# A softmax bound by its transfers: one late load issued 25 rows later, and a row over 126 and 2 partitions moved from the second load to the first store

## The chip, the cores and the metric

The kernel runs on one core of a Trainium2 chip. The metric is device time in microseconds (us); a profile shows the span of the core, about 1.3 us shorter. All runs quoted are of the state fast, and the granted clock of the profiled ones is 1.0. A few executions of the kernel before take 161.1 to 161.6 us instead of about 160.3 (6 of the 44 on record); they count as they are.

## The reference

```python
def reference(x):                       # x: 16 x 1024 x 512, float32
    x_scaled = x / 2.0
    x_max = np.max(x_scaled, axis=-1, keepdims=True)
    exp_x = np.exp(x_scaled - x_max)
    return (exp_x / np.sum(exp_x, axis=-1, keepdims=True)).astype(np.float32)
```

33.55 MB go in and 33.55 MB come out. Per partition there are 128 rows of 512 floats (2,048 B).

## The kernel before

The rows are cut into eight tiles of 3, 5, 15, 25, 25, 25, 20 and 10 rows per partition. The kernel's buffer in SBUF, the on-chip memory, holds 98 rows per partition, so tiles 6 and 7 take the places of tiles 0 to 3 once those are stored. ScalarE takes the exponential of a row and its sum, VectorE multiplies by the reciprocal, SyncE issues the stores. (The kernel's second path, with the maximum taken off, does not run on this data.)

```python
TILES = [(3, 0), (5, 3), (15, 8), (25, 23), (25, 48), (25, 73), (20, 0), (10, 20)]  # rows, place
LATE = {6: (0, 1, 2), 7: (3,)}      # late load: the stores that it waits for
SPREAD = 1
TURN = 73

def load(eng, t):
    r = tiles[t][1]
    parts = [(0, P, 0, r)]
    if t == SPREAD:
        parts = [(0, P, 0, r - 1), (0, 126, r - 1, r), (126, P, r - 1, r)]
    for p, q, lo, hi in parts:
        eng.dma_start(out=sb(t)[p:q, lo:hi], in_=dram(xf, t)[p:q, lo:hi]).then_inc(ld[t], 16)

def store(eng, t):
    eng.wait_ge(s_mul, upto[t])
    eng.dma_start(out=dram(of, t), in_=sb(t)).then_inc(sem_of.get(t, s_end), 16)
# ... ScalarE:
exponentials(straight, TURN)
for t, us in LATE.items():
    nc.scalar.wait_ge(s_home[t], landings(us))
    load(nc.scalar, t)
exponentials(TURN, n_rows)
```

## Time and profile before

| | before |
|---|---|
| time, median of 4 runs | 160.31 us (159.86 to 160.5) |
| span of the profile | 158.9 us |
| bytes moved, mean rate | 67.13 MB, 422 GB/s |
| late loads issued at | 72.9 and 101.0 us |
| last three stores issued at | 122.9, 134.8 and 140.7 us |

The prediction below shows the lines that carry this. Two things help in reading them. The row "DMA" has the busy tenths of the 16 DMA engines in 40 slices. And in the lists of DMA queues, q1 is the ring of SyncE (load 0 and all stores), q10 that of ScalarE (the other loads).

### The profile page before, as it was taken

The numbers are of one execution on the slowest core, as the hardware profiler recorded it, in microseconds if no ns is written. First come the engines' busy times: TensorE is split into PE (matmuls) and PEld (weight loads), VectorE is DVE, ScalarE is ACT, GpSimd is POOL, SyncE is SP. The second block draws the span as 40 slices with busy tenths as digits, with TensorE's granted clock in tenths as the row PEclk, the third lists the DMA queues.
The fourth block names the chain that finished last, engine by engine and source line by source line (L and its number), as shares of the span: only waits on it lengthen the run. The fifth ranks groups of instructions, "written<-read, shape, count | busy, mean of one in ns | idle before, by whom it ended". The sixth has DMA issues, their size and how long they took to land. (4 is left out here: it accounts for less than half of the span.)

```text
span 158.9 us, 665 instructions
## 1 busy us (share of the span) xinstructions
PE 0.2 (0%) x2; PEld 0.1 (0%) x2; DVE 75.1 (47%) x43; ACT 80.3 (51%) x257; POOL 0.2 (0%) x4
## 2 busy tenths in 40 slices
PE   0000000000000000000000000000000000000000
PEld 0000000000000000000000000000000000000000
DVE  0056008920499922989400000007899999960000
ACT  0870498009998089990000000399999999100000
POOL 0000000000000000000000000000000000000000
DMA  7999999799699998999999898997999999999996
GB/s 267 392 487 419 487 462 439 304 477 495 294 410 459 454 510 351 438 428 412 425 480 456 371 552 356 397 541 340 449 418 405 505 412 412 412 454 402 464 387 275
DMA packets 2450, 67.13 MB, mean 422 GB/s; under 512 B 272, under 2 KB 272, under 8 KB 656
## 3 DMA queue, kind: packets, MB, share of 16 engines
q1 hardware_dynamic: 1296, 34.34, 50.5%
q10 hardware_dynamic: 1152, 32.77, 48.4%
q14 instruction: 2, 0.02, 0.0%
HBM read 33.55 MB, written 33.55 MB: 422 GB/s over the span
## 5 line engine op out<-in xcount | busy, mean ns | idle before, releaser
L274 ACT ACTIVATE arena<-arena x125 | 76.6, 614 | 50.6 <-ACTq L135 50.6
L167 DVE TENSOR_TENSOR arena<-arena,recip 128x2560 f32<-128x2560 f32 (+2 forms) x19 | 71.3, 3752 | 0.7
L164 DVE RECIPROCAL recip<-stats 128x5 f32<-128x5 f32 (+2 forms) x19 | 3.7, 195 | 63.1 <-ACT arena L274 57.9
L274 ACT ACTIVATION_READ_ACCUMULATOR arena<-arena x125 | 23.3, 187 | 0.0
L195 ACT ACT_TABLE_LOAD x1 | 1.3, 1283 | 4.7 <-issue 4.7
L199 ACT ACTIVATE arena<-arena 128x512 f32<-128x512 f32 x3 | 1.9, 618 | 0.0
L160 DVE MEMSET ones<- 128x1 f32 x1 | 0.1, 59 | 2.7 <-PEq L35 2.7
L199 ACT ACTIVATION_READ_ACCUMULATOR arena<-arena 128x1 f32 x3 | 0.6, 186 | 0.0
L191 PE MATMUL total<-ones,count 128*1 128x1 f32 x2 | 0.2, 164 | 141.5 <-DVE count L179 141.5
L176 DVE TENSOR_TENSOR inside<-inside,stats 128x128 f32<-128x128 f32 x1 | 0.3, 291 | 0.0
L179 DVE TENSOR_REDUCE count<-inside 128x1 f32<-128x128 f32 x1 | 0.3, 285 | 0.0
L182 DVE TENSOR_SCALAR flag<-total 1x1 int32<-1x1 f32 x1 | 0.1, 147 | 0.3 <-PE total L191 0.3
L172 DVE TENSOR_SCALAR inside<-stats 128x128 f32<-128x128 f32 x1 | 0.2, 220 | 0.0
L191 PEld LDWEIGHTS total<-ones,count 128*1 128x1 f32 x2 | 0.1, 80 | 141.5 <-DVE count L179 141.5
L309 POOL MEMSET const-bfloat16-1.0<- 128x1 bf16 x1 | 0.1, 102 | 0.0
L309 POOL MEMSET const-uint8-127<- 128x1 uint8 x1 | 0.1, 102 | 0.0
L309 POOL MEMSET const-float32-1.0<- 128x1 f32 x1 | 0.1, 99 | 0.0
L309 POOL MEMSET const-float32-0.0<- 128x1 f32 x1 | 0.1, 98 | 0.2 <-issue 0.2
## 6 DMA issues: line engine op xcount, KB each, us to landing
arena<-in_x_dram ACTq DMA_DIRECT2D x3, 6400.0 KB, 52.3
out_dram<-arena SPq DMA_DIRECT2D x3, 6400.0 KB, 44.4
arena<-in_x_dram ACTq DMA_DIRECT2D x1, 5120.0 KB, 36.7
out_dram<-arena SPq DMA_DIRECT2D x1, 5120.0 KB, 18.1
arena<-in_x_dram ACTq DMA_DIRECT2D x1, 3840.0 KB, 15.0
out_dram<-arena SPq DMA_DIRECT2D x1, 3840.0 KB, 39.9
arena<-in_x_dram ACTq DMA_DIRECT2D x1, 2560.0 KB, 24.6
out_dram<-arena SPq DMA_DIRECT2D x1, 2560.0 KB, 18.2
```

Of the source, the lines that this page charges most:

```text
L160: nc.vector.memset(ones[:, :], 1.0).then_inc(s_ones, 1)
L164: nc.vector.reciprocal(out=recip[:, b : b + c], in_=stats[:, b : b + c])._wait_ge(s_exp, ks[-1] + 1).then_inc(s_rec, 1)
L167: nc.vector.tensor_mul(out=arena[:, a : a + c], in0=arena[:, a : a + c], in1=recip[:, b : b + c].unsqueeze(2).to_broadcast([P, c, D]),)._w ...
L172: nc.vector.tensor_scalar(out=inside[:, :], in0=stats[:, :], scalar1=LO, scalar2=HI, op0=Alu.max, op1=Alu.min,).then_inc(s_cnt, 1)
L176: nc.vector.tensor_tensor(out=inside[:, :], in0=inside[:, :], in1=stats[:, :], op=Alu.is_equal)._wait_ge(s_cnt, 1).then_inc(s_cnt, 1)
L179: nc.vector.reduce_sum(out=count[:, :], in_=inside[:, :], axis=mybir.AxisListType.X)._wait_ge(s_cnt, 2).then_inc(s_cnt, 1)
L182: nc.vector.tensor_scalar(out=flag[:, :], in0=total[:, :], scalar1=float(N), scalar2=float(n_rows // G), op0=Alu.is_ge, op1=Alu.mult,)._wa ...
L191: nc.tensor.matmul(total[:, :], lhsT=count[:, :], rhs=ones[:, :], start=True, stop=True)._wait_ge(s_cnt, 3).then_inc(s_tot, 1)
L195: nc.scalar.preload_act_table(Exp)
L199: ins = nc.scalar.activation(out=arena[:, b], in_=arena[:, b], func=Exp, scale=0.5, accum_out=stats[:, b : b + 1],)
L274: ins = nc.scalar.activation(out=data, in_=data, func=Exp, scale=0.5, accum_out=stats[:, r : n_rows - E + 1 + r][:, bass.ds(now, 1)],)
L309: nc = _bacc.Bacc("TRN2", target_bir_lowering=False, num_devices=1)
```

## The change

Load 7 used to be issued directly behind load 6, at row 73, and ScalarE stood still until store 3 had landed; now ScalarE first does tile 5 (rows 73 to 97). And the row that goes out in pieces of 126 and 2 partitions is one of store 0, no longer one of load 1.

```diff
-SPREAD = 1
-TURN = 73
+SPREAD = 0
+TURNS = {6: 73, 7: 98}
     def load(eng, t):
-        ... (three parts if t == SPREAD)
+        eng.dma_start(out=sb(t), in_=dram(xf, t)).then_inc(ld[t], 16)
     def landings(ts):
-        return 16 * len(list(ts))
+        return 16 * sum(3 if t == SPREAD else 1 for t in ts)
     def store(eng, t):
         eng.wait_ge(s_mul, upto[t])
-        eng.dma_start(out=dram(of, t), in_=sb(t)).then_inc(sem_of.get(t, s_end), 16)
+        parts = [(0, P, 0, r)]
+        if t == SPREAD:
+            parts = [(0, P, 0, r - 1), (0, 126, r - 1, r), (126, P, r - 1, r)]
+        for p, q, lo, hi in parts:
+            eng.dma_start(... [p:q, lo:hi] ...).then_inc(sem_of.get(t, s_end), 16)
-        exponentials(straight, TURN)
+        done = straight
         for t, us in LATE.items():
+            exponentials(done, TURNS[t])
             nc.scalar.wait_ge(s_home[t], landings(us))
             load(nc.scalar, t)
-        exponentials(TURN, n_rows)
+            done = TURNS[t]
+        exponentials(done, n_rows)
```

More of the change, by code (lines that the diff above doesn't have):

```diff
@@ L108, in load, with landings, store @@
     def load(eng, t):
+        eng.dma_start(out=sb(t), in_=dram(xf, t)).then_inc(ld[t], 16)
+    stored_by = {u: s_home[t] for t, us in LATE.items() for u in us}
+    for t, (_, r, at) in enumerate(tiles):
+        over = {u for u, (_, ru, au) in enumerate(tiles[:t]) if at < au + ru and au < at + r}
+        assert over <= {u for v, us in LATE.items() if v <= t for u in us}
+    def landings(ts):
+        return 16 * sum(3 if t == SPREAD else 1 for t in ts)
+    near = len(tiles) - 2
+    sem_of = {**stored_by, near: s_near}
+    at_end = landings(t for t in range(len(tiles)) if t not in sem_of)
+    def store(eng, t):
+        eng.wait_ge(s_mul, upto[t])
         r = tiles[t][1]
@@ L114, in load @@
             eng.dma_start(
-                out=sb(t)[p:q, lo:hi], in_=dram(xf, t)[p:q, lo:hi]
-            ).then_inc(ld[t], 16)
-    stored_by = {u: s_home[t] for t, us in LATE.items() for u in us}
-    for t, (_, r, at) in enumerate(tiles):
-        over = {u for u, (_, ru, au) in enumerate(tiles[:t]) if at < au + ru and au < at + r}
-        assert over <= {u for v, us in LATE.items() if v <= t for u in us}
-    def landings(ts):
-        return 16 * len(list(ts))
-    near = len(tiles) - 2
-    sem_of = {**stored_by, near: s_near}
-    at_end = landings(t for t in range(len(tiles)) if t not in sem_of)
-    def store(eng, t):
-        eng.wait_ge(s_mul, upto[t])
-        eng.dma_start(out=dram(of, t), in_=sb(t)).then_inc(sem_of.get(t, s_end), 16)
+                out=dram(of, t)[p:q, lo:hi], in_=sb(t)[p:q, lo:hi]
+            ).then_inc(sem_of.get(t, s_end), 16)
     def take(eng, sem, n):
@@ L188, in program @@
         for t in range(len(tiles)):
-            nc.tensor.wait_ge(ld[t], 48 if t == SPREAD else 16).then_inc(s_go, owner.count(t))
+            nc.tensor.wait_ge(ld[t], 16).then_inc(s_go, owner.count(t))
         nc.tensor.wait_ge(s_ones, 1)
```

## The prediction

> **What bounds the kernel now.** I read the page first, its list of engines and its row of DMA slices.
>
> ```profile
> PE 0.2 (0%) x2; PEld 0.1 (0%) x2; DVE 75.1 (47%) x43; ACT 80.3 (51%) x257; POOL 0.2 (0%) x4
> ...
> DMA  7999999799699998999999898997999999999996
> ...
> DMA packets 2450, 67.13 MB, mean 422 GB/s; under 512 B 272, under 2 KB 272, under 8 KB 656
> ...
> q1 hardware_dynamic: 1296, 34.34, 50.5%
> q10 hardware_dynamic: 1152, 32.77, 48.4%
> ```
>
> No compute engine is busy more than 51% of the 158.9 us span, and the two queues' packets together take 50.5 + 48.4 = 98.9% of the time of 16 DMA engines. q1 is SyncE's ring (first load and all stores), q10 ScalarE's (all other loads). The bound is the DMA engines. The packet records agree: laid over each other, they leave about 1.3 engine-averaged us without a packet in the first 4 us (1.02 of it before the first packet), about 0.1 us between 4 and 156 us, and 0.5 us of uneven finish at the end, with another 0.45 us from the last packet to the span's end. So all that any reordering could win back is about 2 us of 159, most of it at a start that the change hardly touches.
>
> Then the waits, because both halves of the change act on waits.
>
> ```profile
> DVE recip L164 <- ACT arena L274: 57.9, 8, 30.9
> ACT arena L274 <- ACTq L135: 50.6, 5, 30.3
> ```
>
> ScalarE idles once for 30.3 us. The timeline shows why:
>
> ```profile
> 72.92 28.37 ACTq L114 DMA_DIRECT2D arena<-in_x_dram  x2
> ...
> 101.81 0.63 ACT L274 ACTIVATE arena<-arena  x1 [30.26 <-ACTq L135]
> ```
>
> The two late loads, tiles 6 and 7, are issued one behind the other at row 73. ScalarE's order of instructions stands still between them, because tile 7 waits for the store of tile 3, which lands at about 101. Tile 5 (rows 73 to 97) had landed at 82.3 by the arrivals on its semaphore, so its exponentials are about 19 us late. But nothing runs dry for it: DMA stays at 9 or 8 tenths there. That long wait is not on the path that sets the end.
>
> Last, the packets by queue from 20 to 40 us:
>
> ```profile
> DMA packets 320, 8.65 MB, mean 432 GB/s; under 512 B 32, under 2 KB 32, under 8 KB 81
> ...
> q10 hardware_dynamic: 160, 7.37, 85.9%
> q1 hardware_dynamic: 160, 1.27, 15.1%
> ```
>
> Both queues served 160 packets, but q10 moved six times the bytes. A packet is one partition's run of one transfer (51,200 B for 25 rows, 6,144 for 3), and the queues alternate packet by packet. A store cut small therefore advances slowly beside a load of long runs.
>
> **What the Trainium skill says.** "DMA: Bandwidth & Descriptors", section "Queues, rings and completion order": each DMA engine round-robins between queue rows, at packet granularity. The equal 160 and 160 agree. Section "Why a DMA increments its semaphore by 16 and not by 1": the number of engines is the largest one up to 16 that divides the slowest dimension on both sides, and the lowest-numbered are taken; a DMA on fewer has the remainder added by the sequencer. So 126 partitions use 14 engines (9 packets each) and 2 partitions use 2. The trace agrees on the counts: load 1's semaphore has 34 arrivals, 16 + 14 + 2 from engines and two early ones from the sequencer; which engines they were it does not tell. Section "Where 436 GB/s comes from": 435.2 GB/s is the ceiling of the 16 ports. The trace fits: a 51,200 B packet takes about 1.89 to 1.93 us, 26.6 to 27.1 GB/s each, 425 to 434 for sixteen. At that ceiling 67.1 MB take 154.2 us, an estimate from the page, 4.7 under the span.
>
> **Part one: the spread row moves from load 1 to store 0.** Removed: two of ScalarE's first three DMA issues (0.66 and 0.24 us). Its table load, at 4.70, starts perhaps 1 us earlier, but the first exponential waits for load 0 (5.7), so at most 0.2 us is won there. Data costs per engine, with the mean time of a packet: load 1 now takes 8 x 315 + 8 x 88 ns = 3.22 us; in one piece, at the 385 ns that store 1's 10,240 B packets take, 3.08. Store 0 now takes 8 x 234 = 1.87 us; in pieces, 8 x 160 (estimate for 4,096 B at the same rate) + 8 x 88 = 1.98. Sum: -0.14 + 0.11 = -0.03 us. The packet totals even come out equal (q1 +144, q10 -144, 2,450 in all), and each engine's total bytes are the same before and after. Work of the bound: nothing.
>
> What moves is the order. Today store 0 has 8 packets per engine. After: 8 of two rows, plus 9 of one row on 14 engines (10 on two of them), 17 or 18, and still 8 on the two engines that the 126 rows leave out. Each takes a turn against a load packet. Its first turn comes at about 13.4; two rounds lie beside load 2's packets (1.13 + 0.16), the other 15 beside 51,200 B packets (1.9 + about 0.12 = 2.0):
>
> - Store 0 on 14 engines ends at 13.4 + 2.6 + 30 = 46, where it now ends at 27.4 (one engine at 29.7).
> - Store 1, 8 rounds of 1.89 + 0.385: 64, now 46 to 49.
> - By then 23 of the 24 packets of loads 3 to 5 are through on these engines, so store 2 runs alone: 8 x 1.14 = 9.1, plus the last load packet 1.9: 75 to 76, now 70.9 (one engine 72.9).
> - The two left-out engines keep today's schedule: there load 5 still ends at about 80, and a landing counts all 16. So loads 3, 4 and 5 land when they do now (35, 56, 82).
>
> Load 6, which waits for stores 0 to 2, is issued at about 76, not 72.9. SyncE's ring meanwhile holds store 3 (issued at 56.6) and, from 77.2, store 4, each 15.1 us of work for every engine, so none starves. Store 3, in rounds of 1.89 + 1.52 beside load 6, lands at about 101 as now.
>
> **Part two: load 7 at row 98.** ScalarE takes tile 5 as soon as it lands: 82.4 to 97.7 (25 x 0.612). Then store 3 is home at about 101, and load 7 is issued there, within 1 us of now: the row is no longer what holds it. Store 5 is issued at about 101.5, not 122.9. Load 6 lands at about 109.5: exponentials to 122, store 6 issued at 125 (now 134.8). Load 7 lands at about 125.5: its 10 rows take 6.1 us and VectorE 3 more, store 7 issued at about 134.8 (now 140.7). So VectorE's last work moves about 6 us ahead. But stores leave in ring order: store 6 now starts moving at 139.4 and store 7 at 151.5, 4.6 and 10.8 us after their issues. That slack is already there and now doubles. Gain at the end: 0. The one spot where the ring is now empty, 122.3 to 124.1 between stores 4 and 5, is covered by load 7's packets (idle 0.01 us). Gain there: 0.
>
> Sum: -0.03 us of packets, at most -0.2 at the start, up to +0.2 for more turns of tiny store packets: about -0.1. I take 160.3 us.
>
> **Rivals.** (1) A new wait: store 0's slow landing delays load 6 so much that the rings run dry. For it: store 0 gets over twice the turns and load 6 waits for it. Against: stores 3 and 4 stand in the ring from 56.6 and 77.2, so load 6 would have to come after 105 to leave a hole. It would cost the length of the hole; at a hole of 4 us, 164. (2) The opened chain pays: ScalarE's 30.3 us wait goes, VectorE's unbroken tail from 114 to 140.6 loosens, and the end comes earlier. For it: the chain that ended last goes through that tail. Against: the DMA slices stay full and stores 6 and 7 wait for the ring, not for VectorE. At best it gives the 0.5 us of uneven finish: 159.9. (3) The mix counts: 51,200 B loads took 1.91 to 1.93 us beside small stores and 1.89 beside large ones. Eight packets of load 5 moving from the second mix to the first on 14 engines cost 0.3 us: 160.7.
>
> **Range and chances.** A time outside 2% (under 157.3 or over 163.7) needs a hole of 3 us in a stream that has none, or more than all that idles today. 160.3, with 159.6 to 161.0 from the three runs' own spread (160.16 to 160.5), rivals 2 and 3 and some for another chip. Faster 0.01, same 0.97, slower 0.02.
>
> **What would show it.** q1 with 1,440 packets and q10 with 1,008, both shares still about 99% together; in the window 20 to 40 us q1's share down from 15% to about 7%. Store 0's last piece landing about 36 us after issue instead of 19.7, store 1 about 50 (34.2), load 6 issued at 75 to 77. ScalarE's longest wait down from 30.3 to 10 to 13 us, and store 7 issued at 133 to 137. If loads 3 to 5 land much earlier than 35, 56 and 82, the 126 rows were spread over all engines and my account of two unslowed ones is wrong. If any slice of the DMA row from 10 to 150 us falls clearly below today's, rival 1 holds and the time is over 161.

## The result, and the profile after

The changed kernel took **161.51 us** (161.42 to 161.7, 4 runs) against 160.31 before: a ratio of 1.0081, 95% interval 1.0056 to 1.0105. Ratios here and below compare one kernel's fast runs with those of the other in the same rounds, so they are not quite the ratio of the medians quoted. It is within 2%, as given, but slower and outside the range of 159.6 to 161.0. A second series on another chip gave 161.5 us again (1.0074, 1.0057 to 1.009).

The page after: first the engines' and queues' lines.

```profile
DMA  7999999999999979999989999999899999899993
...
DMA packets 2450, 67.13 MB, mean 419 GB/s; under 512 B 272, under 2 KB 272, under 8 KB 656
...
q1 hardware_dynamic: 1440, 34.34, 50.1%
q10 hardware_dynamic: 1008, 32.77, 48.0%
```

The packets are as counted, and the row shows no hole: before the last slice none is under 7 tenths, and before the change one was at 6. What stands out is the last slice: 3 tenths, where it was 6.

The waits of ScalarE after (who waited for whom: total us, times, longest):

```profile
ACT arena L276 <- ACTq L135: 54.0, 6, 12.7
```

The longest wait fell from 30.3 to 12.7 us, as intended. The timeline from 60 us on (start, us, engine, line, operation; in brackets the idle time before) shows tile 5's first exponential at 82.37, load 7's issue at 101.30, and tile 6's first exponential:

```profile
76.74 0.34 ACTq L109 DMA_DIRECT2D arena<-in_x_dram  x1
...
82.37 0.63 ACT L276 ACTIVATE arena<-arena  x1 [11.03 <-ACTq L135]
...
101.30 0.35 ACTq L109 DMA_DIRECT2D arena<-in_x_dram  x1
...
110.47 0.63 ACT L276 ACTIVATE arena<-arena  x1 [12.68 <-ACTq L135]
```

The queues from 20 to 40 us after:

```profile
DMA packets 348, 8.63 MB, mean 432 GB/s; under 512 B 32, under 2 KB 32, under 8 KB 179
...
q10 hardware_dynamic: 174, 8.09, 93.8%
q1 hardware_dynamic: 174, 0.54, 6.7%
```

The rings still take turns packet by packet, and store 0's small packets hold q1 to 6.7% of the time. All of this went as predicted. So where did 1.5 us of span come from? The view by stretches shows it at the end (columns: stretch, length, busy time of PE, PE's weight loads, VectorE, ScalarE and GpSimd, clock, DMA share, GB/s; a packet counts where it starts). Before:

```profile
157.00:158.00 1.00, 0.00 (x0) 0.00 (x0) 0.00 (x0) 0.00 (x0) 0.00 (x0) 1.00 0.46 193
158.00:159.00 1.00, 0.00 (x0) 0.00 (x0) 0.00 (x0) 0.00 (x0) 0.00 (x0) 1.00 0.00 0
159.00:160.00 1.00, 0.00 (x0) 0.00 (x0) 0.00 (x0) 0.00 (x0) 0.00 (x0) 1.00 0.00 0
```

After:

```profile
157.00:158.00 1.00, 0.00 (x0) 0.00 (x0) 0.00 (x0) 0.00 (x0) 0.00 (x0) 1.00 0.31 131
158.00:159.00 1.00, 0.00 (x0) 0.00 (x0) 0.00 (x0) 0.00 (x0) 0.00 (x0) 1.00 0.14 61
159.00:160.00 1.00, 0.00 (x0) 0.00 (x0) 0.00 (x0) 0.00 (x0) 0.00 (x0) 1.00 0.10 41
```

From 157 to 158 fewer packets start than before (193 and 131 GB/s): most engines are done earlier. Then 61 GB/s over 1 us are three packets of the last store (20,480 B each), and 41 GB/s are two. A few engines are late, the others wait for them.

**Which engines.** The trace does not name a packet's engine, but it can be followed: on one engine a packet starts 3 or 4 ns before its predecessor is recorded as ended, and each engine must have its share of each transfer in ring order. This divides the packets of a trace into 16 chains. Up to 8 us, where all engines run within tens of ns of each other, the division is less certain, and a swap of two chains in the same state does not change the list of ends, but it can change which of them belongs to a left-out engine. A second division, made to check this one, gave the same figures for the changed kernel on both chips; for the kernel before it put the left-out engines at 157.96 and 158.44, no less level with the others. In the changed kernel two chains have no packet of 2,048 B at all: those are the two engines that the 126 rows leave out. From the packets, in us:

```
                      the two with the latest start          the other 14
                      first packet    last packet ends       last packet ends
kernel before         1.96, 1.98      157.58, 158.44         157.59 to 158.44
changed kernel        1.68, 1.69      159.85, 159.98         157.32 to 158.20, one 159.26
changed, 2nd chip     1.69, 1.69      158.49, 160.16         157.32 to 157.80, one 159.57
```

The first packets of the other chains start at 1.0 to 1.4. In all three, the two that start last are the two that the 126 rows leave out. They have 18 KB less to move than the others (4.178 and 4.196 MB) and yet end last in the changed kernel (on the second chip one of them does, and the other was less late).

Counting the span from these chains: the mean end of the 16 engines is 157.90 before and 157.97 after, +0.07. The last engine ends 0.54 after the mean before and 2.01 after, +1.47. From the last packet to the end of the span it is 0.45 and 0.39, -0.06. The sum is +1.48, the difference of the spans. The work is the same; its end has become uneven.

**What makes those engines late.** Most packets of 51,200 B take exactly 1,891 ns. On the late engines some take more. The packets of one left-out engine of the changed kernel between 110 and 126 us (S store, L load, start, duration in ns), and of one that is not late:

```
late      S@110.4 1993  L@112.4 761  S@113.1 2299  L@115.4 761  S@116.2 2058  L@118.3 761  S@119.0 1981  L@121.0 761  S@121.7 2561
not late  S@109.3 1891  L@111.2 761  S@112.0 1891  L@113.8 761  S@114.6 1891  L@116.5 761  S@117.2 1891  L@119.1 761  S@119.9 1891
```

After 8 us, packets took 3.3 and 3.5 us over the usual duration on the two left-out engines (1.3 and 1.4 of it from 112 to 126 us), 2.2 on the third late one, and 0.6 to 1.2 on the others. I call such packets stretched. Before, the two left-out engines had 0.7 and 1.5 (1.0 and 1.5 in the second division). Stretching is not theirs alone: before, three of the other engines had 0.8 to 1.1 us of it from 112 to 126 us.

### The profile page after: what moved, and what is told of

Same layout as the page of the kernel before. It is cut to its first block, busy times and chain, and to the rows that moved or that the text cites.

```text
span 160.4 us, 668 instructions
## 1 busy us (share of the span) xinstructions
PE 0.2 (0%) x2; PEld 0.1 (0%) x2; DVE 75.6 (47%) x43; ACT 80.4 (50%) x257; POOL 0.2 (0%) x4
## 3 DMA queue, kind: packets, MB, share of 16 engines
q1 hardware_dynamic: 1440, 34.34, 50.1%
q10 hardware_dynamic: 1008, 32.77, 48.0%
## 6 DMA issues: line engine op xcount, KB each, us to landing
arena<-in_x_dram ACTq DMA_DIRECT2D x1, 5120.0 KB, 33.4
```

## The experiments

Each kernel was timed in five rounds beside the kernel before, the last in three. Kernels of one series ran on one chip: the first four, the next four, the next four (the changed kernel again to load 7 at row 98 with a row of the last store), and the last. I began with three theories. A: the left-out engines run out of step because store 0's pieces leave them out. B: the later half, with load 7 at row 98, costs. C: store 0's extra turns and the later load 6 cost.

### Load 7 at row 98 alone

```diff
 (kernel before)
-TURN = 73
+TURNS = {6: 73, 7: 98}          # and the loop over LATE as in the change
```

> The kernel before with load 7 moved to row 98 alone; the spread row stays with load 1. Theory A (the two engines that store 0's 126 rows leave out run out of step with the others, some of their packets are stretched, and they finish late): 160.3 us, within 0.4 of before; last stores' landings spread over about 1 us as before. Theory B (the later part of the change costs: tile 5 and load 7 in a new order between 82 and 125 us): about 161.5. Theory C (the extra turns of store 0 and the load 6 that comes 3.8 us later cost, whichever engines have them): 160.3.

160.81 us (160.29 to 161.1), ratio 1.0015 (0.9989 to 1.0042). The profile (159.8 us, on the slowest of the six runs) has one late engine, a left-out one, ending at 159.37 against 158.01 at most on the others. This engine had 2.4 us of stretched packets, although the row of load 1 had relieved it early. Not the whole loss, and not clearly any.

### The spread row in store 0 alone

```diff
 (changed kernel)
-TURNS = {6: 73, 7: 98}
+TURNS = {6: 73, 7: 73}          # an empty range of rows is skipped
```

> The changed kernel with both late loads at row 73 again; store 0 keeps its three pieces. Theory A: 161.5 us, and the final landings again in two groups, 13 engines within 1 us and two or three some 1.5 to 2 us later. Theory B: 160.3. Theory C: 161.5.

161.15 us (159.98 to 161.51), ratio 1.0034 (0.9999 to 1.0069). Four of six runs lie at 161.1 to 161.5. The profile fell on one of 160.5: its left-out engines end at 158.01 and 158.42, level with the others. So this half can lose about as much as the whole change, but doesn't always; the groups that A expected were not in the one run profiled.

### Store 0 in two even pieces

```diff
 (changed kernel)
-            parts = [(0, P, 0, r - 1), (0, 126, r - 1, r), (126, P, r - 1, r)]
+            parts = [(0, P, 0, r - 1), (0, P, r - 1, r)]      # and 2 landings, not 3
```

> The changed kernel with store 0 in two pieces of 128 partitions (2 rows, then 1 row): as many store packets on 14 engines as in the changed kernel, but all 16 engines have them, none is left out. Theory A: 160.3 us or a little less, one group of final landings, and loads 3, 4 and 5 landing at about 34, 50 and 68 us on all engines. Theory B: 161.5. Theory C: 161.5 or more, since load 6 comes as late (about 76).

161.5 us (161.39 to 161.53), ratio 1.0064 (1.004 to 1.0089). No engine is left out; loads 3 to 5 landed at 33.4, 51.0 and 71.9 (34.6, 55.6 and 82.1 in the changed kernel), where A said 34, 50 and 68. And yet two engines end at 159.70 and 159.78, the other 14 by 158.01. These two are again the ones with the last first packet (1.77 and 1.79), and they trail: load 5 reached them at 71.6 and 71.9, the others by 69.9. A is refuted: being left out of store 0 is not the cause.

### No split at all, load 7 at row 98

```diff
 (changed kernel)
-SPREAD = 0
+SPREAD = None
```

> The changed kernel with no transfer split at all, load 7 at row 98. Theory A: 160.3 us, one group of final landings. Theory B: 161.5. Theory C: 160.3, with load 6 issued at about 71 to 73 us.

161.72 us (161.54 to 162.1), ratio 1.008 (1.0053 to 1.0106). A and C, which said 160.3, fall here: neither pieces nor extra turns nor a late load 6 (it came at 73.0) are there, and it is as slow. The end of this kernel:

```profile
158.00:159.00 1.00, 0.00 (x0) 0.00 (x0) 0.00 (x0) 0.00 (x0) 0.00 (x0) 1.00 0.19 82
159.00:160.00 1.00, 0.00 (x0) 0.00 (x0) 0.00 (x0) 0.00 (x0) 0.00 (x0) 1.00 0.10 41
```

The chains say more. Two engines have their first packet at 1.70 and 1.72, the others at 1.0 to 1.3. From the arrivals on the loads' semaphores, two trail all the way: at load 2 they are at 17.7 and 17.8 where the others are at 16.7 to 17.2, at load 5 at 83.2 and 83.2 against 80.1 to 80.6. They end at 160.30 and 160.33, the others by 158.09. (The profile fell on a run of 162.06.)

That made a new theory, **D**: two engines start about 0.7 us late in every run. They are the two that 126 rows leave out. In the kernel before, the split row of load 1 takes 16 KB off exactly these, 0.6 us, right after the late start. Without it they trail, trailing engines get stretched packets, and they set the end. Its rival E: stretching strikes at random, and which engine is last is chance.

### No split, both late loads at row 73

```diff
 (kernel without split)
-TURNS = {6: 73, 7: 98}
+TURNS = {6: 73, 7: 73}
```

> No transfer split, both late loads at row 73: the missing corner between the kernel before (161 with neither, so far) and the unsplit kernel at row 98 (161.7). Theory D (two engines get their first packet some 0.7 us late in every run; they are the two that 126 rows leave out; engines that trail the others get stretched packets, above all between 112 and 126 us when store 5 already stands behind store 4; those few set the end): 160.5 to 161, the trailing two caught up in part at 124 us, where the row-73 order stretches packets of the others. Theory E (the stretching falls on engines at random and each kernel's time is only its sum): the same as the unsplit kernel at row 98, 161.7.

161.92 us (161.18 to 162.33), ratio 1.0068 (1.0024 to 1.0112). D missed with 160.5 to 161: the row-73 order does not let the trailing engines catch up. The two late starters end at 159.64 and 160.20, a third at 159.91. So without the split in load 1 the kernel is slow with either order, and B can't be the cause of it.

### The last row of the last store over 126 and 2 partitions

```diff
 (changed kernel)
-SPREAD = 0
+SPREAD = 7
```

> The unsplit kernel at row 98, with the last row of the last store (tile 7) over 126 and 2 partitions: nothing moves before the last store, but the two left-out engines have 16 KB less (8 packets of 2,048 B, 0.6 us). Theory D: they end 0.6 us sooner, so 161.1 against 161.7. Theory E: 161.7, as each engine is as likely as another to be last.

160.94 us (160.83 to 161.19), ratio 1.0013 (0.9972 to 1.0053), 0.78 under the kernel without split, on another chip, where D said 0.6. Up to the last store it is that kernel; only the two engines have less to do at its end. Its end:

```profile
158.00:159.00 1.00, 0.00 (x0) 0.00 (x0) 0.00 (x0) 0.00 (x0) 0.00 (x0) 1.00 0.09 39
159.00:160.00 1.00, 0.00 (x0) 0.00 (x0) 0.00 (x0) 0.00 (x0) 0.00 (x0) 1.00 0.00 0
```

No packet starts after 159. The two late starters end at 158.82 and 159.19. E, which said no change, does not fit: the engines that 126 rows leave out are those that set the end. Not all of the difference between the two profiles is the relief, though: store 6 had already landed at 153.7 and 154.1 on the two, against 154.6 and 154.7 in the profile without the split.

### Three rows of the last store

```diff
 (as the last)
-            parts = [(0, P, 0, r - 1), (0, 126, r - 1, r), (126, P, r - 1, r)]
+            parts = [(0, P, 0, r - 3), (0, 126, r - 3, r), (126, P, r - 3, r)]
```

> As the last, with three rows: 49 KB or 1.8 us less on the two engines, 0.23 us more on the others (0.46 on two). Theory D: the two end at about 158.5 to 158.9, level with the others; 160.0 to 160.3 against 161.7 for the unsplit kernel. Theory E: 161.7 to 162.

160.88 us (160.78 to 161.35), ratio 1.0016 (0.9975 to 1.0057). Less than hoped: 1.8 us of work less, but no gain over one row. The packets show why: of the 128 of 14,336 B, 122 take 535 ns, and four that start late, from 155.8 to 157.6, take 748 to 1,325. The last two engines are stretched once more, 1.9 us between them, while the others are at their small pieces. About half of the relief was given back.

### Two rows of load 1, load 7 at row 98

```diff
 (kernel before with load 7 at row 98)
-            parts = [(0, P, 0, r - 1), (0, 126, r - 1, r), (126, P, r - 1, r)]
+            parts = [(0, P, 0, r - 2), (0, 126, r - 2, r), (126, P, r - 2, r)]
```

> The kernel before with load 7 at row 98 and two rows of load 1 over 126 and 2 partitions, where the one-row form gave 160.8 with one trailing engine. Theory D: 1.3 us of relief at the start against 0.7 us of lateness, so the two engines lead instead of trailing, are not stretched, and the end is level: 159.8 to 160.3. Theory E: 160.8.

160.92 us (160.49 to 161.02), ratio 1.0006 (0.9966 to 1.0047). In the profile, which fell on the run of 160.49, the two left-out engines had first packets at 1.87 and 2.07, but now lead: they end at 157.07 and 157.11, first of all, with no more than 0.04 us of stretching after 8 us (3.3 and 3.5 in the changed kernel). So in this profile the trailing and its stretching go when the late start is made up for, and these two engines are not simply slower ones. The time is over the 159.8 to 160.3 that D expected; four of the runs lie at 160.85 to 161.02, and no profile shows one of them.

### The changed kernel again, and with one row of the last store as well

```diff
 (changed kernel)
-SPREAD = 0
+SPREAD = (0, 7)                  # and "t in SPREAD" for "t == SPREAD"
```

> The changed kernel unaltered, as the measure for the three runs beside it on the same chip. Both theories: 161.5 us, as on the first chip; final landings of 13 engines within 1 us and three 1.5 to 2.5 us later.

> The changed kernel, with the last row of the last store over 126 and 2 partitions as well. Theory D (the two engines that start late, which the 126 rows leave out, trail and set the end): those two lose 0.6 us of work, and the third trailing engine of the first profile keeps its end at about 159.3, so 160.9 to 161.0, 0.5 to 0.6 under the changed kernel. Theory E (which engine is last is chance): no change, 161.5.

Unaltered: 161.5 us (161.24 to 161.88), with three late engines, of which one left-out one was less late this time (table above). With the row of the last store: 161.03 us (160.85 to 161.43), 0.47 less, ratios 1.0074 and 1.0051. D said 0.5 to 0.6. The loss in the changed kernel itself thus sits at its late engines.

### Two rows of load 1 with both late loads at row 73

```diff
 (kernel before)
-            parts = [(0, P, 0, r - 1), (0, 126, r - 1, r), (126, P, r - 1, r)]
+            parts = [(0, P, 0, r - 2), (0, 126, r - 2, r), (126, P, r - 2, r)]
```

> The kernel before with two rows of load 1 over 126 and 2 partitions instead of one, both late loads at row 73. Theory D: the two late starters lead, as they did with this split at row 98, so 160.3 to 160.9 and none of the runs of 161.4 and more that the kernel before sometimes shows. Theory E: the same two kinds of run as before has, some 160.3 and some 161.5.

160.97 us (160.4 to 162.38), ratio 1.0059 (1.0028 to 1.009). A miss for D: no steadier than the kernel before, and slower. Its profile again has the two late starters ending first (156.87 and 157.08) and the others by 158.58, in a span of 159.1; what makes other runs longer is not seen there. One row is enough; two give nothing.

### Load 7 at row 98 and a row of the last store

```diff
 (kernel before with load 7 at row 98)
+LAST = 7                         # store 7 in the three parts of load 1, 3 landings for it
```

> The kernel before with load 7 at row 98 and the last row of the last store over 126 and 2 partitions too. Its one trailing engine (159.4 in the profile of the kernel with row 98 alone, against at most 158.0 on the others) was a left-out one, so theory D: 0.6 us sooner, 160.0 to 160.3 against 160.8. Theory E: 160.8.

160.23 us (160.01 to 160.51), ratio 0.9996 (0.9979 to 1.0013), where row 98 alone had 160.81 on another chip. This is as D said: the one late engine of row 98 alone was a left-out one. But the intervals of the two ratios overlap. Here the row-98 order costs nothing against the kernel before, but gains nothing either. It is the best of the versions tried, level with the kernel before.

### Less work for the compute engines (wrong results on purpose)

What stretches the trailing engines' packets? One suspect, SBUF traffic of ScalarE and VectorE, can be taken away.

```diff
 (kernel without split, load 7 at row 98)
+            w = 64 if owner[ks[0]] in LATE else D         # columns of VectorE's multiplication
+                ... 0 : 64 if first == 98 else D ...        # columns of ScalarE's exponentials
```

> The unsplit kernel at row 98, with exponentials and multiplications of tiles 6 and 7 on 64 of 512 columns only (wrong results on purpose), so that ScalarE and VectorE hardly touch SBUF from 110 us on; the transfers are the same. In the unsplit kernel two trailing engines had packets of store 4 stretched by 0.2 to 0.55 us each between 112 and 122 us, about 1.4 us per engine. Theory F (the compute engines' SBUF traffic stretches them): no such packets, the last landing at about 159.2, 160.3 us. Theory G (the transfers do it to one another): the same stretched packets, 161.7 us.

161.62 us (161.47 to 161.93), ratio 1.0084 (1.0067 to 1.0101). The stretch from 110 to 126 us, first of the kernel without split, then of this one:

```profile
110.00:126.00 16.00, 0.00 (x0) 0.00 (x0) 11.75 (x8) 12.36 (x40) 0.00 (x0) 1.00 0.96 410
```

```profile
110.00:126.00 16.00, 0.00 (x0) 0.00 (x0) 2.72 (x8) 4.29 (x34) 0.00 (x0) 1.00 0.95 409
```

VectorE is busy 2.7 us instead of 11.75, ScalarE 4.3 instead of 12.4, and the time stays. The two trailing engines still have 0.8 and 0.9 us of stretching from 112 to 126 us (1.4 and 1.5 with full work) and end at 159.79 and 159.83. The compute engines add at most a part, and even that is not shown: in the kernel with one row of the last store, which does the full work and has the same transfers up to there, the two had 0.9 and 1.2. What it is among the transfers that stretches a trailing engine's packets is **open**.

## Why the prediction was wrong

**Right, by its own steps.** q1 1,440 and q10 1,008 packets; q1's share from 20 to 40 us 6.7% (7 was said). The two left-out engines keep the pace of before, so loads 3 to 5 land at 34.6, 55.6 and 82.1 (35, 56, 82). Store 0's last piece lands at 49.4, 38.3 us after its issue (36). Load 6 is issued at 76.7 (75 to 77), load 7 at 101.3 (101). ScalarE's longest wait is 12.7 (10 to 13). No hole, so rival 1 is out; ScalarE's longest wait is shorter (its waits in total are not: 54.0 us against 50.6) and brings no time, so rival 2 is out. Rival 3 is too small: the summed packet time per engine rose from 157.16 to 157.32 us, and the mean end of the engines by 0.07 us.

**Off without effect.** Store 7 was to be issued at 133 to 137; it was at 142.4. Load 7 landed at 132.7, not 125.5: store 5 stood in the ring behind store 4, so its last packets went on taking turns with 51,200 B packets, and the trailing engines had it last of all. Store 7's first packet moved at 151.25 in any case, so this slack held.

**The step that failed** is the conclusion of part one: "each engine's total bytes are the same before and after. Work of the bound: nothing", together with the uneven finish, which I took for a fixed 0.5 us that could only be won. I added up the work of the average engine, and that sum was right. But the kernel ends with its last engine, and the last minus the mean went from 0.54 to 2.01 us. That term, +1.47, is the whole error.

**What the runs showed in its place.** I had read the row over 126 and 2 partitions as a shape of equal cost wherever it stands. It is a correction: the two engines that it leaves out are those with the late first packet. In load 1 it comes at once, and the two run level with the others. Moved to store 0, the same 16 KB are saved, but from 14 us on, when the engines are already trailing. In bytes that still pays for the late start. For a left-out engine of the changed kernel the first packet comes about 0.6 us later than on the others, and the 18 KB less to move are worth about 0.7 us (an estimate at the pace of 51,200 B in 1.891 us). What is left is the stretching, 3.3 and 3.5 us against 0.6 to 1.2 on most others, and it is about the 2.4 us by which these two end after the median of the others. The kernels in one table (medians; the series ran on different chips, each beside the kernel before, whose median was 160.3 to 160.5):

| split row | both late loads at row 73 | load 7 at row 98 |
|---|---|---|
| load 1 | 160.3 (before) | 160.8 |
| store 0 (126 and 2) | 161.15 | 161.5 (changed) |
| store 0, even pieces | - | 161.5 |
| none | 161.9 | 161.7 |
| last store | - | 160.9 |
| last store, three rows | - | 160.9 |
| store 0 and last store | - | 161.0 |
| load 1, two rows | 161.0 | 160.9 |
| load 1 and last store | - | 160.2 |

Down the columns, the time falls where the two late engines are relieved by one row early, or at the very end. Two rows early give no more, and at row 73 they are slower than one (1.0059, 1.0028 to 1.009); why is not known. Across the rows, the order at row 98 has no clear price: +0.5, +0.35 and -0.2, and its own ratio, 1.0015, holds 1 within its interval.

What is shown: the loss is the late finish of a few engines, above all the left-out ones (the chains; the two runs that relieve them at the end alone, with 0.78 and 0.47 us less). That the late start begins it is supported by two rows in load 1, which make the same two engines finish first, and by every unsplit trace; it was not removed at its source, and no run relieved two other engines for comparison. Nor is an early relief always enough: with row 98 and the row of load 1, one left-out engine still ended at 159.37. Why trailing packets are stretched, and why the kernel before has an execution of 161.1 to 161.6 now and then, stays open; none of those was profiled.

## What to carry to other kernels

Where a kernel keeps its DMA engines full, count the end by the last engine and not by the mean: look at the last slices of the DMA row, and at how far apart the 16 arrivals on the last semaphore are. An odd-looking split in a tuned kernel may be a balance weight; ask which engines it leaves out, and whether those are late, before moving it. Here one row of relief paid early, before the engine fell out of step, and in part at the very end; in store 0 it was eaten up.

## What the Trainium skill lacked or had wrong

- "DMA: Bandwidth & Descriptors", section "Latency and other measured facts", says that engines 7 and 15 are usually slower, with a guess that concerns SWDGE. Here all transfers are issued by SyncE and ScalarE, and two engines get their first packet at 1.7 to 2.1 us, in the profiles that could be divided, where nearly all the others have it at 1.0 to 1.4. Both are among those that 126 partitions leave out, so by the page's rule for the lowest-numbered engines they would be 14 and 15; the trace has no numbers.
- The same page, section "SWDGE vs HWDGE vs iDMA", has a packet of preferably at most 4,096 B, where it describes what GpSimd builds (SWDGE). No page says how large the packets of SyncE's and ScalarE's transfers are. In these traces a packet, as the profile records it, is one partition's whole run, up to 51,200 B and 1.89 us, and the turn between rings is that long.
- The same page, section "Queues, rings and completion order", describes the turns between rings but not that the completion write takes a turn of its own: a packet of 4 B and 9 ns, with a packet of the other ring before and after it, as at the end of store 0 in the changed kernel.
- No page has the stretching: in the changed kernel, on the engines that trail the others, 51,200 B packets took up to 0.7 us over 1.89 between 112 and 122 us, while nearly all packets of the other engines kept to 1.891; up to 3.5 us were lost on one engine over the run.
- The rule for the number of engines of a DMA (section "Why a DMA increments its semaphore by 16 and not by 1") held: 126 rows ran on 14 engines with 9 packets each, and 2 rows on two of these 14.
